# Attention layer of a two-layer decoder trunk: four engines issue in source order instead of the scheduler's order

## Chip, core and metric

The kernel runs on one core of a Trainium2 chip. The metric is the device time of one execution in microseconds (us); smaller is better. Three runs of the kernel before gave 1360.05 to 1361.44 us, median 1360.51 us.

## What is computed

A decoder trunk of two pre-normalised residual layers over one sequence of 512 tokens, D = 1024, each followed by a dense SwiGLU layer. The first layer mixes with a recurrence (a gated linear recurrence beside a state-space mixer), the second with dilated window attention. The change is in the attention layer, which in the reference reads, cut:

```python
def attention_layer(x, norm_g, w_qkv, q_norm, k_norm, w_out):
    h = rmsnorm(x, norm_g)
    qkv = (h @ w_qkv).reshape(b, l, 3, ATT_HEADS, ATT_HEAD_DIM)      # 16 heads of 64
    q = partial_rope(rmsnorm(qkv[:, :, 0], q_norm), pos) * (ATT_HEAD_DIM ** -0.5)
    k = partial_rope(rmsnorm(qkv[:, :, 1], k_norm), pos)
    v = qkv[:, :, 2]
    for window, dilation in DILATED_PATTERNS:                        # (128,1) (512,4) (2048,16)
        o_i, m_i, d_i = dilated_window_attention(q, k, v, window, dilation)
        ...
    o = jnp.sum(wts[..., None] * jnp.stack(outs), axis=0) / jnp.sum(wts, axis=0)[..., None]
    return x + o @ w_out
```

and around it, for layer 0 and 1: `x = mixer(x)`, then `x = x + (silu(g) * u) @ w_down` with `g, u = split(rmsnorm(x) @ w_gate_up)`. Everything is float32. The kernel folds the three windows into one softmax per row over all 512 keys, with a table of logarithmic counts (`lnc`) added to the scores.

## The kernel before, in words

Activations stand transposed, as eight tiles of 128 channels x 512 tokens. Float32 products are made from three matmuls of split operands: every operand is kept as a rounded high part and the rest as a low part (`xh`, `xl`; `wh`, `wl`; `ph`, `pl`; `qk_hi`, `qk_lo`). `split` (L87 to L89) makes such a pair: ACT casts the high part (L88), DVE subtracts it (L89). A weight tile of 128 x 1024 is loaded by SP (L110, three buffers `wr`) and split into `wh` and `wl` (three buffers each), two tiles ahead of its use.

PE does all matmuls, ACT casts, squares and exponentials, DVE most elementwise work, POOL (GpSimd) a few powers and the division of the probabilities. In time the layers are: recurrent layer, its feed-forward layer, attention (about 723 to 1006 us of the profiled execution), second feed-forward layer.

In the attention layer the source is written as a hand-made interleaving. Large projections are cut into *pieces* of about 1.4 us of PE work, kept in the list `pieces`; `fill_in(n)` issues n of them between the small, dependent steps of the heads, and runs what was put off with `later` (so many pieces later) or `after_piece` (after the next fill). Pieces and steps:

- `qk_pieces`: six matmuls `ps_qkv` (L762 to L764) a piece, 16 pieces for four heads' q and k. Their end: ACT `q` and `qsq` (L773, L775); two pieces later DVE `qss` (L784, L785) and POOL `qrs`, a power (L786); six pieces later DVE `q` scaled by `qrs` (L790); seven and eight later the rotary part `rc`, `rs` (L801, L802) and two additions (L806, L807).
- `v_pieces`: twelve matmuls `ps_v` of 256 columns (L827 to L829), 8 pieces; the last four evacuate, ACT `v` (L836) and DVE `v` (L837). `ps_qkv`, `ps_v` and `ps_ao` share four PSUM buffers.
- `pair_T`: PE transposes `ps_qT` (L849), ACT `qk_hi` (L852), DVE `qk_lo` (L853).
- `scores(p, b)`, b = 0, 1, 2: PE `ps_s` (L873), DVE adds `lnc` and takes the row extreme (L884, `s,m`), ACT exponential (L885); then, after the next fill, `quotients`: DVE reciprocal (L890) and POOL's product `s` (L892).
- `turn(h, b)`: PE transposes the probabilities, `ps_pT` (L900), then ACT `ph` and DVE `pl`. `turn(h, 0)` reads all four row blocks of head h and so needs the quotients of all three score groups.
- `values(h, b)`: PE `ps_o` from `pl` (L915) and `ph` (L916); at its end ACT `bot` (L923) and DVE `o` (L926) and the split into `xh`, `xl`.
- `ao_pieces`: output projection, six matmuls `ps_ao` (L117 to L119) a piece, DVE adds to `x` (L950).

The loop runs over eight pairs of heads, p = 0 to 7, twelve steps each: turns and values of the pair (ha, hb), and between them `pair_T` and `scores` of the next pair. Pairs 0 to 4 have twelve pieces, one a step (p = 0, 2, 4: the last four qk pieces of a group and its eight v pieces; p = 1, 3: twelve qk pieces); pairs 5, 6 and 7 have only 4, 5 and 4 `ao` pieces for twelve steps.

Tiles carry the dependences, and semaphores are put in for them. The order in which an engine issues is not that of the source: the scheduler of the tile framework picks, engine by engine, among what is ready by its own estimate. Each engine then issues its own list in that order, and an instruction that waits holds up all that stands behind it on its engine.

Of the kernel before, what the change touches and what calls it, by code (L numbers as in the profile page):

```python
# [25 lines left out]
HID = ((0, 8), (8, 15), (15, 22))  # L26
XBC = 12
NEG = -1e30


_PV = {}
# [27 lines left out]
def trunk(ctx: ExitStack, tc: tile.TileContext, a):  # L59
# [185 lines left out]
    norm = Norm("rec_norm")  # L245
# [11 lines left out]
    with ExitStack() as rctx:  # L257
# [390 lines left out]
        norm = Norm("ffn_norm0", (8, 9, 10, 11, 4, 5, 6, 7))  # L648
# [38 lines left out]
    norm = norm2  # L687
    norm3 = Norm("ffn_norm1", (8, 9, 10, 11, 4, 5, 6, 7))
    with ExitStack() as actx:
# [34 lines left out]
        queue = []  # L724
# [86 lines left out]
        def v_pieces(g):  # L811
            pss = []

            def piece(vp, t):
                i = i_qkv[g, 4 + vp]
                if t == 0:
                    w_cur[i] = weight_get(i)
                if vp == 0:
                    pss.append(pa.tile([P, T], F32, tag="pa", name="ps_v"))
                wh, wl = w_cur[i]  # L820
                ts_ = slice(t * P, (t + 1) * P)
                ps = pss[t][:, :256]
                for k4 in range(4):
                    k = 4 * vp + k4
                    xh, xl = norm.hl[k]
                    cols = slice(k4 * 256, (k4 + 1) * 256)
                    mm(ps, lhsT=xl[:, ts_], rhs=wh[:, cols], start=(k == 0), stop=False)  # L827
                    mm(ps, lhsT=xh[:, ts_], rhs=wl[:, cols], start=False, stop=False)
                    mm(ps, lhsT=xh[:, ts_], rhs=wh[:, cols], start=False, stop=(k == KD - 1))  # L829
                if t == 2:  # L830
                    weight_emit(i + AHEAD)
                if vp == 1:
                    v = ap_.tile([P, 4, 2, 64], F32R, tag=f"v{t}", name="v", bufs=2)
                    r = norm.rt[:, t:t + 1]
                    pv3 = ps.rearrange("p (h e) -> p h e", h=4)
                    S.activation(v[:, :, 0], pv3, AF.Copy, scale=r)  # L836
                    V.scalar_tensor_tensor(out=v[:, :, 1], in0=pv3, scalar=r, in1=v[:, :, 0].bitcast(F32), op0=ALU.mult, op1=ALU.subtract)  # L837
                    vt[g, t] = v

            return [lambda vp=vp, t=t: piece(vp, t) for vp in range(2) for t in range(NT)]  # L840
# [3 lines left out]
        def pair_T(p, w):  # L844
            g, pp = p // 2, p % 2
            o = w * 256 + pp * P
            ps = pm.tile([P, T], F32, tag="pm", name="ps_qT")
            for t in range(NT):
                nc.tensor.transpose(ps[:, t * P:(t + 1) * P], qk[g][:, t].rearrange("p h e -> p (h e)")[:, o:o + P], ident)  # L849
            hi = ap_.tile([P, T], F32R, tag=f"hi{w}", name="qk_hi", bufs=2)  # L850
            lo = ap_.tile([P, T], F32R, tag=f"lo{w}", name="qk_lo", bufs=2)
            S.activation(hi, ps, AF.Copy, scale=gains[w])  # L852
            V.scalar_tensor_tensor(out=lo, in0=ps, scalar=gains[w], in1=hi.bitcast(F32), op0=ALU.mult, op1=ALU.subtract)  # L853
            qkT[p, w] = (hi, lo)
# [9 lines left out]
        def scores(p, b):  # L864
            (qh, ql), (kh, kl) = qkT[p, 0], qkT[p, 1]
            pss = [pm.tile([P, T], F32, tag="pm", name="ps_s") for _ in range(2)]
            for i, c in S_AT[b]:
                n = (i + 1) * P
                qs = slice(i * P, (i + 1) * P)
                for z, (ql_, kr) in enumerate(((qh, kl), (ql, kh), (qh, kh))):  # L870
                    for e in range(2):
                        rows = slice(64 * e, 64 * e + 64)
                        mm(pss[e][:, c:c + n], lhsT=ql_[rows, qs], rhs=kr[rows, :n], start=(z == 0), stop=(z == 2))  # L873
            k = 2 * len(S_AT[b])
            m = am.tile([P, 3, 4], F32, tag="m", name="m", bufs=6)
            done = []
            for i, c in S_AT[b]:
                n = (i + 1) * P
                for e in range(2):
                    if c == 0:  # L880
                        prob[2 * p + e, "s", b] = at.tile([P, WID[b]], F32, tag=f"s{b}", name="s", bufs=4)
                    s, ps = prob[2 * p + e, "s", b][:, c:c + n], pss[e][:, c:c + n]
                    u = len(done)
                    V.tensor_tensor_reduce(out=s, in0=ps, in1=lnc[:, T - n:], scale=-1.0, scalar=-NEG, op0=ALU.add, op1=ALU.min, accum_out=m[:, 0, u:u + 1])  # L884
                    S.activation(s, s, AF.Exp, scale=-1.0, bias=m[:, 0, u:u + 1], accum_out=m[:, 1, u:u + 1])  # L885
                    prob[2 * p + e, i] = s
                    done.append(s)

            def quotients():
                V.reciprocal(m[:, 2, :k], m[:, 1, :k])  # L890
                for u, s in enumerate(done):
                    G.tensor_scalar(out=s, in0=s, scalar1=m[:, 2, u:u + 1], scalar2=1.0, op0=ALU.mult, op1=ALU.mult)  # L892

            after_piece.append(quotients)
# [39 lines left out]
        def ao_pieces(half, after=None):  # L934
            st = {}

            def piece(mp, m2, kk):
                i = i_ao[half, mp]
                if m2 == 0 and kk == 0:
                    w_cur[i] = weight_get(i)  # L940
                if kk == 0:
                    st["ps"] = pa.tile([P, T], F32, tag="pa", name="ps_ao")
                for k in (2 * kk, 2 * kk + 1):
                    c = (m2 * 4 + k) * P
                    mm3(st["ps"], w_cur[i], oT[4 * half + k], (slice(None), slice(c, c + P)), (slice(None), slice(None)), k == 0, k == 3)
                if m2 == 0 and kk == 1:
                    weight_emit(i + AHEAD)
                if kk == 1:
                    m = 2 * mp + m2
                    V.tensor_tensor(out=x[m], in0=st["ps"], in1=x[m], op=ALU.add)  # L950
                    if after is not None:
                        after(m)

            return [lambda mp=mp, m2=m2, kk=kk: piece(mp, m2, kk) for mp in range(4) for m2 in range(2) for kk in range(2)]
# [3 lines left out]
        def fill_in(n=1):  # L958
            for _ in range(min(n, len(pieces))):
                pieces.pop(0)()  # L960
                tick()
            ready = after_piece[:]
            after_piece.clear()
            for f in ready:
                f()


        pieces += qk_pieces(0)
        fill_in(4)
        norm.finish()  # L970
        fill_in(12)
        pieces += v_pieces(0)
        fill_in(8)
        pieces += qk_pieces(1)
        fill_in(2)
        pair_T(0, 0)
        pair_T(0, 1)
        fill_in(3)
        for b in range(3):
            scores(0, b)  # L980
            fill_in(2)
        fill_in(1)
        for p in range(8):
            g = p // 2
            if p % 2 == 0 and g < 3:
                pieces += v_pieces(g + 1)
            elif p % 2 == 1 and g < 2:
                pieces += qk_pieces(g + 2)
            elif p == 5:
                pieces += ao_pieces(0)  # L990
            n = [12, 12, 12, 12, 12, 4, 5, 4][p]
            nxt = p < 7
            ha, hb = 2 * p, 2 * p + 1
            steps = [
                [lambda: turn(ha, 0)],
                [lambda: turn(ha, 1)] + ([lambda: pair_T(p + 1, 0)] if nxt else []),
                [lambda: values(ha, 0), lambda: turn(ha, 2)],
                [lambda: values(ha, 1)] + ([lambda: pair_T(p + 1, 1)] if nxt else []),
                [lambda: values(ha, 2)],
                [lambda: turn(hb, 0)],  # L1000
                [lambda: scores(p + 1, 0)] if nxt else [],
                [lambda: values(hb, 0), lambda: turn(hb, 1)],
                [lambda: scores(p + 1, 1)] if nxt else [],
                [lambda: values(hb, 1), lambda: turn(hb, 2)],
                [lambda: scores(p + 1, 2)] if nxt else [],
                [lambda: values(hb, 2)],
            ]
            for k, fs in enumerate(steps):
                for f in fs:
                    f()  # L1010
                fill_in(n * (k + 1) // 12 - n * k // 12)
        fill_in(len(pieces))
        assert not queue
        pieces += ao_pieces(1, norm3.feed)
        fill_in(len(pieces))

    def store(m):
        nc.sync.dma_start(out=a["out"][m], in_=x[m])
# [98 lines left out]
```

## Time and profile before

| | us |
|---|---|
| median of three runs | 1360.51 |
| the profiled execution | 1360.34 |
| its span, first to last instruction | 1358.5 |
| PE busy | 1323.7 (97%) |
| DVE busy | 779.4 (57%) |
| ACT busy | 553.3 (41%) |
| POOL busy | 74.8 (6%) |
| attention layer, from 723 to 1006 us: PE busy of 283.0 | 266.05 |

PE's share is near the whole span, so time is lost or won where PE stands still or runs at a lower clock. "Idle before <- releaser" in a row is how long the engine had stood, and whose end set it free. The clock column is the granted TensorE clock as a share of 2.4 GHz.

### The profile page before, as it was taken

Reading aid. Unit: us, or ns where it says so; the run is one execution under the profiler, and the core shown is the slowest. Engines: PE = TensorE matmul, PEld = TensorE weight load, DVE = VectorE, ACT = ScalarE, POOL = GpSimd, SP = SyncE. Lnnn points to the kernel's source line nnn. Section 1 sums busy time; section 2 is a strip of 40 time slices with the busy share of each in tenths; the row PEclk is TensorE's granted clock in tenths of the full one; section 3 lists DMA queues with packets and bytes.
Section 4 is the critical chain, followed back from the end, with each engine's and each line's share of the span. In section 5 each row is a group of like instructions: output and inputs, shape, how many; then the busy total and the mean of one; then the engine's idle time right before and its main releaser. Section 6 shows DMA issues by size and latency. Waiting matters only on the chain.

```text
span 1358.5 us, 16006 instructions
## 1 busy us (share of the span) xinstructions
PE 1323.7 (97%) x6314; PEld 1086.0 (80%) x6314; DVE 779.4 (57%) x1264; ACT 553.3 (41%) x818; POOL 74.8 (6%) x94
## 2 busy tenths in 40 slices
PE   7999989999999999999999889989999999999998
PEld 6877767788888888888888778777788888888887
DVE  6887799975544434434465575767754434443442
ACT  6743867433333222222244466556543212222321
POOL 0000000000000000000001232232100000000000
PEclk9999989999999999999999999999999999999999
DMA  6322322532333333332332211211133332233332
GB/s 237 110 89 82 94 78 85 164 95 94 96 94 103 94 93 102 87 107 94 95 97 87 78 48 62 63 47 47 63 93 94 95 106 94 89 97 105 97 90 81
DMA packets 38555, 126.53 MB, mean 93 GB/s; under 512 B 4288, under 2 KB 5056, under 8 KB 38352
## 3 DMA queue, kind: packets, MB, share of 16 engines
q1 hardware_dynamic: 38480, 125.51, 29.9%
q8 instruction: 49, 0.80, 0.2%
q14 instruction: 26, 0.21, 0.0%
HBM read 123.36 MB, written 2.13 MB: 92 GB/s over the span
## 4 chain that ended last, share of the span: by engine, by line
PE 86%; DVE 6%; ACT 4%; POOL 2%; issue 1%; DMA 0%; SPq 0%; POOLq 0%; ACTq 0%; DVEq 0%
PE ps_pr L117 24%; PE ps_pr L118 24%; PE ps_pr L119 24%; PE ps_qkv L762 2%; POOL qrs L786 2%; PE ps_qkv L764 2%; PE ps_qkv L763 2%; PE ps_ao L119 1%; PE ps_ao L117 1%; PE ps_ao L118 1%; DVE wl L89 1%; PE ps_s L873 1%; PE ps_pT L900 1%; ACT s L885 1%; DVE qss L784 1%
## 5 line engine op out<-in xcount | busy, mean ns | idle before, releaser
L88 ACT CAST wh<-wr 128x1024 fp32r<-128x1024 f32 (+2 forms) x223 | 228.3, 1024 | 609.6 <-PE ps_pr L119 389.3
L117 PE MATMUL ps_pr<-xh,wl 128*128 128x512 f32 x1056 | 416.9, 395 | 13.6 <-DVE wl L89 12.1
L118 PE MATMUL ps_pr<-xl,wh 128*128 128x512 f32 x1056 | 414.6, 393 | 0.0
L119 PE MATMUL ps_pr<-xh,wh 128*128 128x512 f32 x1056 | 413.5, 392 | 0.0
L89 DVE TENSOR_TENSOR wl<-wr,wh 128x1024 fp32r<-128x1024 f32 (+2 forms) x223 | 265.3, 1190 | 76.4 <-ACT wh L88 75.6
L117 PEld LDWEIGHTS ps_pr<-xh,wl 128*128 128x128 f32 x1056 | 199.4, 189 | 56.4 <-DVE wl L89 13.0
L119 PEld LDWEIGHTS ps_pr<-xh,wh 128*128 128x128 f32 x1056 | 199.4, 189 | 42.3 <-issue 0.7
L118 PEld LDWEIGHTS ps_pr<-xl,wh 128*128 128x128 f32 x1056 | 199.5, 189 | 42.0 <-issue 1.1
L119 PE MATMUL ps_pr<-ah,wh 128*128 128x512 f32 x352 | 137.1, 389 | 0.0
L117 PE MATMUL ps_pr<-ah,wl 128*128 128x512 f32 x352 | 137.1, 389 | 0.0
L118 PE MATMUL ps_pr<-al,wh 128*128 128x512 f32 x352 | 137.1, 389 | 0.0
L671 DVE TENSOR_TENSOR tu<-ps_pr,nrb 128x512 f32<-128x512 f32 x44 | 30.4, 691 | 130.7 <-PE ps_pr L119 130.7
L679 DVE TENSOR_TENSOR x<-ps_pr,x 128x512 f32<-128x512 f32 x48 | 33.2, 692 | 122.6 <-PE ps_pr L119 122.6
L669 DVE TENSOR_TENSOR tg<-ps_pr,nrb 128x512 f32<-128x512 f32 x44 | 30.4, 691 | 94.0 <-PE ps_pr L119 94.0
L119 PEld LDWEIGHTS ps_pr<-ah,wh 128*128 128x128 f32 x352 | 66.1, 188 | 13.8
L117 PEld LDWEIGHTS ps_pr<-ah,wl 128*128 128x128 f32 x352 | 66.1, 188 | 13.7
L118 PEld LDWEIGHTS ps_pr<-al,wh 128*128 128x128 f32 x352 | 66.1, 188 | 13.6
L762 PE MATMUL ps_qkv<-wh,xl 128*128 128x512 f32 x128 | 54.3, 424 | 3.9 <-DVE v L837 3.9
L885 ACT ACTIVATE s<-s,m 128x512 f32<-128x512 f32 (+3 forms) x64 | 35.4, 554 | 55.3 <-DVE m L884 55.3
L764 PE MATMUL ps_qkv<-wh,xh 128*128 128x512 f32 x128 | 51.0, 398 | 0.0
L763 PE MATMUL ps_qkv<-wl,xh 128*128 128x512 f32 x128 | 50.6, 396 | 0.0
L892 POOL TENSOR_SCALAR s<-s,m 128x512 f32<-128x512 f32 (+3 forms) x64 | 38.4, 616 | 109.9 <-DVE m L890 84.4
(230 smaller groups left out, 1615.7 us busy)
## 6 DMA issues: line engine op xcount, KB each, us to landing
wr<-in_w_gu SPq DMA_DIRECT2D x88, 512.0 KB, 3.5
wr<-in_w_in SPq DMA_DIRECT2D x35, 512.0 KB, 3.6
wr<-in_w_dn SPq DMA_DIRECT2D x32, 448.0 KB, 3.3
wr<-in_w_qkv SPq DMA_DIRECT2D x24, 512.0 KB, 3.5
wr<-in_w_out SPq DMA_DIRECT2D x16, 512.0 KB, 3.5
wr<-in_w_dn SPq DMA_DIRECT2D x16, 512.0 KB, 3.5
x<-in_xT SPq DMA_DIRECT2D x16, 256.0 KB, 3.6
bcs<-csd SPq DMA_DIRECT2D x16, 256.0 KB, 4.6
```

The lines of the kernel that those rows point to most:

```text
L88: S.copy(hi, src)
L89: V.tensor_tensor(out=lo, in0=src, in1=hi.bitcast(F32), op=ALU.subtract)
L117: mm(ps, lhsT=wl[ws], rhs=xh[xs], start=start, stop=False)
L118: mm(ps, lhsT=wh[ws], rhs=xl[xs], start=False, stop=False)
L119: mm(ps, lhsT=wh[ws], rhs=xh[xs], start=False, stop=stop)
L669: V.tensor_tensor(out=tg, in0=pg, in1=rb, op=ALU.mult)
L679: V.tensor_tensor(out=x[m], in0=ps, in1=x[m], op=ALU.add)
L762: mm(pss[t], lhsT=xl[:, ts_], rhs=wh[:, cols], start=(k == 0), stop=False)
L763: mm(pss[t], lhsT=xh[:, ts_], rhs=wl[:, cols], start=False, stop=False)
L764: mm(pss[t], lhsT=xh[:, ts_], rhs=wh[:, cols], start=False, stop=(k == KD - 1))
L885: S.activation(s, s, AF.Exp, scale=-1.0, bias=m[:, 0, u:u + 1], accum_out=m[:, 1, u:u + 1])
L892: G.tensor_scalar(out=s, in0=s, scalar1=m[:, 2, u:u + 1], scalar2=1.0, op0=ALU.mult, op1=ALU.mult)
```

## The change

Inside the attention layer the body that issues all pieces and steps is put into `with tc.manual_schedule(engines=ORDERED)`, where `ORDERED` is PE, ACT, DVE and POOL: these four issue in the order in which the source makes the instructions. SP, which issues the loads, stays with the scheduler. No instruction is added or removed. The lines after it move by one (before the block) or two (inside it).

```diff
+ORDERED = {mybir.EngineType.PE, mybir.EngineType.Activation, mybir.EngineType.DVE, mybir.EngineType.Pool}
...
-        pieces += qk_pieces(0)
-        fill_in(4)
-        norm.finish()
-        fill_in(12)
...
+        with tc.manual_schedule(engines=ORDERED):
+            pieces += qk_pieces(0)
+            fill_in(4)
+            norm.finish()
+            fill_in(12)
...
+            for p in range(8):
...
+            fill_in(len(pieces))
+            assert not queue
+            pieces += ao_pieces(1, norm3.feed)
+            fill_in(len(pieces))
```

The order of POOL and of SP is the same in both kernels. PE's is the same up to pair 5. DVE and ACT move all through the layer.

DVE, pair 0, around the `pl` of `values(1, 0)`, before (`wl_6036` is the low part of the next weight tile, `q` the scaled q of one token block, `s,m` the scores of pair 1):

```order
L926 TENSOR_TENSOR o<-ps_o,bot 64x512
L784 TENSOR_REDUCE qss<-qsq 128x8
L785 TENSOR_SCALAR qss<-qss 128x8
L89 TENSOR_TENSOR wl_6036<-wr_6034,wh_6035 128x1024
L89 TENSOR_TENSOR pl<-ps_pT,ph 128x512
L790 TENSOR_TENSOR q<-q,qrs 128x512
L884 ISA s,m<-ps_s,cst 128x512
```

and after:

```order
L785 TENSOR_REDUCE qss<-qsq 128x8
L786 TENSOR_SCALAR qss<-qss 128x8
L927 TENSOR_TENSOR o<-ps_o,bot 64x512
L90 TENSOR_TENSOR pl<-ps_pT,ph 128x512
L791 TENSOR_TENSOR q<-q,qrs 128x512
L885 ISA s,m<-ps_s,cst 128x512
...
L90 TENSOR_TENSOR wl_6038<-wr_6036,wh_6037 128x1024
L791 TENSOR_TENSOR q<-q,qrs 128x512
```

The weight's low part moved from ahead of `pl` to behind the scores, and each `q` from right behind its own `qss` to behind all four of them.

DVE, end of pair 0, around the last reciprocal of pair 1's scores, before (`128x256` scores are group b = 2):

```order
L837 SCALAR_TENSOR_TENSOR v<-ps_v,nrt,v 128x4x64
L884 ISA s,m<-ps_s,cst 128x256
L884 ISA m 128x1
...
L890 RECIPROCAL m<-m 128x2
L837 SCALAR_TENSOR_TENSOR v<-ps_v,nrt,v 128x4x64
L926 TENSOR_TENSOR o<-ps_o,bot 64x512
```

and after:

```order
L802 TENSOR_TENSOR rc<-q,rope_c 128x512
L803 TENSOR_TENSOR rs_6145<-q,rope_s 128x512
L885 ISA s,m<-ps_s,cst 128x256
L885 ISA m 128x1
...
L90 TENSOR_TENSOR wl_6177<-wr_6175,wh_6176 128x1024
L838 SCALAR_TENSOR_TENSOR v<-ps_v,nrt,v 128x4x64
L807 TENSOR_TENSOR q<-rc,rs_6145 128x32x8
L808 TENSOR_TENSOR q<-rc,rs_6145 128x32x8
L891 RECIPROCAL m<-m 128x2
```

Four instructions now stand between these scores and their reciprocal: a weight's low part, one `v` and the two rotary additions. On ACT the cast of that weight, `wh_6176`, stands behind the two exponentials of the same scores. At the end of the odd pairs 1 and 3 one weight's low part stands there.

PE, pair 5, from the last scores of pair 6 to `values(11, 2)`, before (`ps_ao` are matmuls of the output projection):

```order
L900 MATMUL ps_pT<-cst,s 128x128 x2
L873 MATMUL ps_s<-qk_lo,qk_hi 128x256 x2
L873 MATMUL ps_s<-qk_hi,qk_lo 128x256 x2
L873 MATMUL ps_s<-qk_hi 128x256 x2
L117 MATMUL ps_ao<-xh_6815,wl_7254 128x512
L118 MATMUL ps_ao<-xl_6816,wh_7253 128x512
L915 MATMUL ps_o<-pl,v 128x256
```

and after:

```order
L901 MATMUL ps_pT<-cst,s 128x128 x2
L874 MATMUL ps_s<-qk_lo,qk_hi 128x256 x2
L874 MATMUL ps_s<-qk_hi,qk_lo 128x256 x2
L874 MATMUL ps_s<-qk_hi 128x256 x2
L916 MATMUL ps_o<-pl,v 128x256
L917 MATMUL ps_o<-ph,v 128x256
L118 MATMUL ps_ao<-xh_6817,wl_7256 128x512
```

The two matmuls of the output projection that stood ahead of the values moved behind them.

## Rows read from the trace of the kernel before

**Rows 1.** The page: busy time, share of the span and instructions by engine.

```profile
PE 1323.7 (97%) x6314; PEld 1086.0 (80%) x6314; DVE 779.4 (57%) x1264; ACT 553.3 (41%) x818; POOL 74.8 (6%) x94
```

**Rows 2.** PE's waits from 720 to 1010 us: total, times, longest.

```profile
PE ps_o L915 <- DVE pl L89: 10.9, 6, 3.1
PE ps_qkv L762 <- DVE v L837: 3.9, 1, 3.9
PE ps_s L873 <- DVE qk_lo L853: 1.6, 3, 0.6
```

**Rows 3.** First long stop: DVE, then PE (start, us, operation, idle before).

```profile
752.00 0.69 DVE L790 TENSOR_TENSOR q<-q,qrs 128x512 f32<-128x512 f32 x1 [1.75 <-POOL qrs L786]
...
755.87 1.65 DVE L837 SCALAR_TENSOR_TENSOR v<-ps_v,nrt,v 128x256 fp32r<-128x256 f32 x4
...
756.40 0.51 PE L762 MATMUL ps_qkv<-wh,xl 128*128 128x512 f32 x1 [3.89 <-DVE v L837]
```

**Rows 4.** Stop in pair 0: DVE, then PE; last row: the same in pair 4.

```profile
796.03 0.68 DVE L89 TENSOR_TENSOR pl<-ps_pT,ph 128x512 fp32r<-128x512 f32 x1
...
791.68 0.40 PE L873 MATMUL ps_s<-qk_hi 64*128 64x512 f32 x2
...
796.77 0.50 PE L915 MATMUL ps_o<-pl,v 128*128 128x512 f32 x1 [3.06 <-DVE pl L89]
...
909.86 0.50 PE L915 MATMUL ps_o<-pl,v 128*128 128x512 f32 x1 [2.92 <-DVE pl L89]
```

**Rows 5.** Stretches: length, busy PE, PEld, DVE, ACT, POOL, clock, DMA share, GB/s.

```profile
756.50:760.50 4.00, 4.00 (x11) 3.13 (x12) 2.15 (x4) 0.00 (x0) 0.00 (x0) 0.57 0.63 158
797.50:805.00 7.50, 7.50 (x53) 7.02 (x52) 7.02 (x20) 4.41 (x13) 2.94 (x3) 0.77 0.24 72
...
951.00:955.00 4.00, 3.03 (x22) 2.17 (x18) 2.64 (x12) 3.04 (x12) 1.50 (x3) 1.00 0.00 0
```

**Rows 6.** End of pair 0: DVE, POOL, PE; then DVE busy (x) in a stretch, clock.

```profile
808.71 0.17 DVE L890 RECIPROCAL m<-m 128x2 f32<-128x2 f32 x1 [0.82 <-ACT s L885]
...
808.97 0.93 POOL L892 TENSOR_SCALAR s<-s,m 128x256 f32<-128x256 f32 x2 [1.21 <-DVE m L890]
...
809.45 0.60 PE L900 MATMUL ps_pT<-cst,s 128*128 128x128 f32 x4
...
798.25:809.60 11.35, 9.13 (x30) 0.86 0.23 78
```

**Rows 7.** End of pair 1: the same chain.

```profile
833.68 0.93 POOL L892 TENSOR_SCALAR s<-s,m 128x256 f32<-128x256 f32 x2 [0.39 <-DVE m L890]
...
834.78 0.60 PE L900 MATMUL ps_pT<-cst,s 128*128 128x128 f32 x4
```

**Rows 8.** Groups from 723 to 965 us by shape: busy, mean ns, idle before.

```profile
L88 ACT CAST wh<-wr 128x1024 fp32r<-128x1024 f32 x27 | 28.3, 1046 | 24.0 <-PE ps_qkv L764 18.0 <-PE ps_v L829 3.6 <-issue 1.8
...
L885 ACT ACTIVATE s<-s,m 128x512 f32<-128x512 f32 x16 | 11.4, 716 | 35.2 <-DVE m L884 35.2
...
L885 ACT ACTIVATE s<-s,m 128x256 f32<-128x256 f32 x16 | 8.0, 502 | 7.7 <-DVE m L884 7.7
...
L89 DVE TENSOR_TENSOR wl<-wr,wh 128x1024 fp32r<-128x1024 f32 x27 | 33.2, 1229 | 20.4 <-ACT wh L88 20.1
...
L790 DVE TENSOR_TENSOR q<-q,qrs 128x512 f32<-128x512 f32 x16 | 11.1, 693 | 26.1 <-POOL qrs L786 26.1
L837 DVE SCALAR_TENSOR_TENSOR v<-ps_v,nrt,v 128x256 fp32r<-128x256 f32 x16 | 7.4, 480 | 1.2 <-ACT v L836 1.1
```

**Rows 9.** Pair 5, last scores and values: PE twice, then DVE.

```profile
936.83 0.50 PE L117 MATMUL ps_ao<-xh,wl 128*128 128x512 f32 x1
...
938.28 0.39 PE L915 MATMUL ps_o<-pl,v 128*128 128x256 f32 x1 [0.72 <-DVE pl L89]
...
940.35 0.15 DVE L890 RECIPROCAL m<-m 128x2 f32<-128x2 f32 x1
```

**Rows 10.** DMA issues: weight tiles of the attention layer, KB each, us to landing.

```profile
wr<-in_w_qkv SPq DMA_DIRECT2D x24, 512.0 KB, 3.5
```

More of the change, by code (lines that the diff above doesn't have):

```diff
@@ L965, in fill_in @@
                 f()
-        pieces += qk_pieces(0)
-        fill_in(4)
-        norm.finish()
-        fill_in(12)
[L972 to L980, printed above, removed]
-            fill_in(2)
[L982 to L1015, printed above, removed]
+        with tc.manual_schedule(engines=ORDERED):
[3 more added lines that the diff above has]
+            fill_in(12)
+            pieces += v_pieces(0)
+            fill_in(8)
+            pieces += qk_pieces(1)
+            fill_in(2)
+            pair_T(0, 0)
+            pair_T(0, 1)
+            fill_in(3)
+            for b in range(3):
+                scores(0, b)
+                fill_in(2)
+            fill_in(1)
+            for p in range(8):
+                g = p // 2
+                if p % 2 == 0 and g < 3:
+                    pieces += v_pieces(g + 1)
+                elif p % 2 == 1 and g < 2:
+                    pieces += qk_pieces(g + 2)
+                elif p == 5:
+                    pieces += ao_pieces(0)
+                n = [12, 12, 12, 12, 12, 4, 5, 4][p]
+                nxt = p < 7
+                ha, hb = 2 * p, 2 * p + 1
+                steps = [
+                    [lambda: turn(ha, 0)],
+                    [lambda: turn(ha, 1)] + ([lambda: pair_T(p + 1, 0)] if nxt else []),
+                    [lambda: values(ha, 0), lambda: turn(ha, 2)],
+                    [lambda: values(ha, 1)] + ([lambda: pair_T(p + 1, 1)] if nxt else []),
+                    [lambda: values(ha, 2)],
+                    [lambda: turn(hb, 0)],
+                    [lambda: scores(p + 1, 0)] if nxt else [],
+                    [lambda: values(hb, 0), lambda: turn(hb, 1)],
+                    [lambda: scores(p + 1, 1)] if nxt else [],
+                    [lambda: values(hb, 1), lambda: turn(hb, 2)],
+                    [lambda: scores(p + 1, 2)] if nxt else [],
+                    [lambda: values(hb, 2)],
+                ]
+                for k, fs in enumerate(steps):
+                    for f in fs:
+                        f()
+                    fill_in(n * (k + 1) // 12 - n * k // 12)
+            fill_in(len(pieces))
+            assert not queue
+            pieces += ao_pieces(1, norm3.feed)
+            fill_in(len(pieces))
```

## Prediction
> **What bounds the kernel now.** I read the page first, then PE's waits in the attention layer, then the rows around each long wait, and last the granted clock behind them. PE is busy 97% of the span and no other engine over 80% [rows 1], so the change can win only where PE stands still or runs slowly inside the layer. PE's waits there [rows 2] are few: one of 3.89 us for a DVE `v` [rows 3], six together 10.9 us for a DVE `pl`, three of 0.6 at most for `qk_lo`. Of the six, three are alike, one each in pairs 0, 2 and 4, of 3.06 us at the first and 2.92 at the last [rows 4]; the three others, in pairs 5 to 7, make up the rest, 2.0.
>
> The long ones have one cause. DVE has put each `q` right behind its own `qss`, and must stand 1.75 us for POOL's power in between [rows 3]; `q` waits 26.1 us in its sixteen places [rows 8]. What PE needs, a `v` or a `pl`, stands behind that. DVE itself has time: it is busy 9.13 of 11.35 us even in the dense stretch at the end of pair 0 [rows 6].
>
> They cost more than their idle time. Behind the first stop the granted clock is a mean 0.57 over 4 us, behind the second 0.77 over 7.5 us [rows 5], levels of 0.5 and 1.0 mixed: 4 x 0.43 and 7.5 x 0.23, about 1.7 us of PE work lost each time. Behind the waits below 1 us near 952 us the clock stayed at 1.00 [rows 5].
>
> **What goes.** PE's order is the same up to pair 5, so until there only DVE's and ACT's orders count. With `qss` of all four token blocks ahead and `q` six pieces behind its square, POOL's power is long done when `q` comes: in the first part the `v` stand in their pieces and the 3.89 us stop goes, with its clock: -3.9 - 1.7 = **-5.6 us**. In pairs 0, 2 and 4 `pl` no longer stands behind a waiting `q` and a weight's low part: -3.0 each, with the `qk_lo` wait of about 0.5 just ahead (1.6 in three, rows 2) and the clock 1.7, which is -5.2 each.
>
> **What comes at the end of pairs 0, 2 and 4.** PE's next turn needs the quotients of all three score groups. In the kernel before this chain is met with nothing to spare: reciprocal 808.71, POOL's first product from 808.97 (two in 0.93), PE's transposes at 809.45 with no wait [rows 6]. In the new order DVE does a weight's `wl`, a `v` and two additions ahead of that reciprocal, and the `wh` that `wl` waits for stands on ACT behind the exponentials. That alone adds, by starts of 0.08 less than the means in [rows 8], 0.97 (`wh`) + 1.15 (`wl`) + 0.40 (`v`) + 0.7 (two additions of half a `q`) = 3.2 us, all of it on the path: the low bound, which supposes that DVE comes to the last scores as early as PE does.
>
> It does not. From the first 512-wide score of the next pair PE needs, to its next turn, 809.45 - 791.68 [rows 4, 6] less the stop of 3.06, the 1.7 of clock and about 0.3 for the first head's share: 12.7 us. DVE has from that score to the reciprocal what it had before from 798.25 to 809.60, 9.13 us [rows 6], and besides `wl` 1.15 and three `q` of 0.61 that stood earlier: 12.1 us. In strict order it also waits three times on ACT. The first `wl` waits for a cast behind two exponentials of 512: 0.7 + 2 x 0.72 + 0.97 against 1.2 of its own work, 2 us. The first `v` waits behind four exponentials, about 1.3. The second `wl` waits for two exponentials of 256 (0.50 each, rows 8) and a cast, 1.8. Sum 17.2, POOL's start and first product 0.7 [rows 6]: 17.9 against PE's 12.7. Stop: **about 5 us**, in one piece at the turn, bounds 2.6 (some slack gained ahead) to 6.5. Such a stop is longer than all those behind which the clock halved, so 1.7 goes with it. Net 5.0 + 1.7 - 5.2 = +1.5 each, **+4.5 us** for three; with 2.6 and no clock loss -7.8, with 6.5 and the clock +9.
>
> The Trainium skill ("TensorE: Matmul & The Clock Gate", What's actually happening) says that the gate watches a free-running window, so whether a given idle time costs the clock depends on where it falls. The trace does not show such luck for the long stops of this layer, both stretches of rows 5 lost 1.7; were the three new ones to escape, the sum below would be lower by 5.1.
>
> **The end of pairs 1 and 3.** One `wh` and one `wl` come between the exponentials and the last reciprocal: 0.97 + 1.15 and some 0.07 of handing over, 2.2. Before, POOL starts at 833.68, half of its 0.93 later the first head's product is there, and PE comes at 834.78 [rows 7]: 0.6 to spare. Stop 1.5 each, **+3.0**. Its length lies between waits that did and did not cost the clock [rows 4, 5]; I take none, bounds +2.0 to +6.4 with it.
>
> **Pairs 5 to 7.** With four or five pieces for twelve steps the scheduler had filled PE's gaps with single `ps_ao` matmuls. In source order they are gone. In pair 5 the last values could be reached at 936.83, where the first `ps_ao` of the filling stands, and could start at 938.28 [rows 9]: 1.4 instead of 0.72. Then one piece, 1.4, and the turn at about 939.9, while the reciprocal is at 940.35 [rows 9] and POOL 0.7 behind [rows 6]: 1.2. `values(ha, 0)` comes with only eight transposes of the other turn and `pair_T` between: cast and `pl`, some 0.68 each [rows 4], against two to three groups of four transposes of 0.60 at most [rows 6]: an estimate of 0.5. Pair 6 has a piece ahead of its last values, so 0.5 + 1.2; pair 7 has no `pair_T` and again none, 0.9 + 0.9. Sum 6.6, against 2.0 before: **+4.5**, bounds +2 and +8 (whole pieces may still cover more, or each of these gaps may lengthen the next).
>
> **At nothing.** No instruction is added. The loads stay in SP's order; `wr` is set free up to 3 us later where its cast stands behind exponentials, but a load lands in 3.5 us [rows 10] and is made two tiles, eight pieces or 11 us, ahead. POOL's order is unchanged, and it is 6% busy [rows 1]. If the cover of the loads failed, a weight would be late by about 1 us a tile at the dense ends of pairs.
>
> **Sum.** -5.6 + 4.5 + 3.0 + 4.5 = +6.4 us on the profiled execution's 1360.34, which is 0.17 under the median: 1366.7, and 1366.9 against the median; I say **1367**. The ends of the terms: -5.6 - 7.8 + 2 + 2 = -9.4, 1351; -5.6 + 9 + 6.4 + 8 = +17.8, 1378.
>
> **Rivals.**
> 1. *Faster.* The four long stops go (12.8 us with 6.8 of clock and 1.6 for `qk_lo`, 21 us in all), and the turn at the end of the even pairs waits only for what is put ahead of the reciprocal. For: DVE's busy share is moderate, and its 1.75 us waits for POOL vanish, which may let it reach the last scores early enough. Against: three waits behind ACT in the new order. With stops of 2.6 to 3.2 that keep the clock the three pairs give -7.8 to -6.0, the rest +1.9: 1354 to 1357. It decides below 3.5 us a stop, clock kept. Chance 0.25.
> 2. *No change that can be measured.* What can be told from none is about 0.2%, 2.7 us. The turn's stop with its clock equals the stop that went, 5.2 (three pairs at 0), or the ends of pairs 1 and 3 and pairs 5 to 7 come out at their low bounds, +4: 1358 to 1363. That the change does nothing, since PE's order moves so little, ends here too; but DVE's order moves at just those places where PE waits. Chance 0.17.
> 3. *Much slower.* The shorter new stops cost the clock too, and the stop of the even pairs is 6.5: up to +17.8, 1373 to 1378. It decides if a stop of 1.5 us is enough for the clock to fall. Chance 0.13.
>
> The forecast (1363 to 1373) has 0.45. Faster 0.25, same 0.17, slower 0.58. The range for 8 in 10 takes in most of the faster case and of the slower ones: 1354 to 1375.
>
> **What would show it.** Right: no wait of PE for `v` near 752 us and none of 3 us for `pl`; in their place PE's `ps_pT` waits for POOL's `s` five times, three times about 5 us and twice 1.5, the clock at half behind the three; DVE's reciprocal there right behind two additions; `q` without waits for POOL; PE waits for `pl` four or five times of 0.5 to 1.4 in pairs 5 to 7. Wrong: a wait for `ps_pT` below 3 us in pair 0 (rival 1), PE waits for weights (`wl`), or for `pl` in the middle of an even pair, which would mean that DVE is late already there.

## The result: slower, 1377.5 us, and the profile after

The changed kernel takes 1377.5 us in the median of four runs (1376.36 to 1379.58), against 1360.84 for the kernel before on the same chip: ratio 1.0125, 95% interval 1.0107 to 1.0142. The prediction was 1367 with 1354 to 1375 as its range. The side was right, the size was not: the span grew by 18.3 us (1358.5 to 1376.8), almost three times the +6.4 of the sum, and the time lies outside the range.

The page of the profile after (busy time, share of the span, instructions), to be read beside [rows 1]:

```profile
PE 1331.5 (97%) x6314; PEld 1091.1 (79%) x6314; DVE 781.3 (57%) x1264; ACT 553.9 (40%) x818; POOL 75.9 (6%) x94
```

The instructions are the same. PE's busy time rose by 7.8 us with the same matmuls, which points to a lower clock; the waits and the clock are added up below. PE's waits in the attention layer (total, times, longest), to be read beside [rows 2]:

```profile
PE ps_pT L901 <- POOL s L893: 19.2, 7, 5.2
PE ps_o L916 <- DVE pl L90: 7.6, 7, 2.4
PE ps_s L874 <- DVE m L885: 1.6, 2, 1.4
```

16.7 us of waits before have become 28.5. The long wait for `v` [rows 3] and the three of 3 us for `pl` [rows 4] are gone, and so are those for `qk_lo`. In their place stands the wait of the next pair's turn for POOL's product, just where the prediction put it. The end of pair 0, to be read beside [rows 6] (start, duration, operation, idle before):

```profile
798.79 0.41 DVE L885 CUSTOM_DVE_ANT_0 s<-ps_s,cst 128x256 f32<-128x256 f32 x1
...
801.30 1.23 DVE L90 TENSOR_TENSOR wl<-wr,wh 128x1024 fp32r<-128x1024 f32 x1 [1.75 <-ACT wh L89]
802.44 0.48 DVE L838 SCALAR_TENSOR_TENSOR v<-ps_v,nrt,v 128x256 fp32r<-128x256 f32 x1
802.84 0.42 DVE L807 TENSOR_TENSOR q<-rc,rs 128x256 f32<-128x256 f32 x1
803.17 0.42 DVE L808 TENSOR_TENSOR q<-rc,rs 128x256 f32<-128x256 f32 x1
803.50 0.16 DVE L891 RECIPROCAL m<-m 128x2 f32<-128x2 f32 x1
...
800.24 1.03 ACT L89 CAST wh<-wr 128x1024 fp32r<-128x1024 f32 x1
...
803.83 0.93 POOL L893 TENSOR_SCALAR s<-s,m 128x256 f32<-128x256 f32 x2 [4.03 <-DVE m L891]
...
804.36 0.90 PE L901 MATMUL ps_pT<-cst,s 128*128 128x128 f32 x3 [5.11 <-POOL s L893]
...
833.32 0.55 PE L901 MATMUL ps_pT<-cst,s 128*128 128x128 f32 x3 [1.30 <-POOL s L893]
```

The last row is the end of pair 1. Read the others upwards from 804.36: PE had stood 5.11 us, POOL's product was released by the reciprocal, and the reciprocal stood behind two additions, a `v` and a `wl` that itself waited 1.75 us for its cast on ACT. The ends of pairs 2 and 4 look the same (5.17 and 5.16), those of pairs 1 and 3 have stops of 1.30 each.

Pairs 5 to 7 hold what the prediction missed: PE's longer stops there, then DVE just ahead of one of them:

```profile
936.74 0.32 PE L874 MATMUL ps_s<-qk_lo,qk_hi 64*128 64x128 f32 x1 [1.35 <-DVE m L885]
...
948.72 0.72 PE L916 MATMUL ps_o<-pl,v 128*128 128x512 f32 x1 [1.66 <-DVE pl L90]
...
959.02 0.78 PE L916 MATMUL ps_o<-pl,v 128*128 128x512 f32 x1 [2.44 <-DVE pl L90]
...
972.92 0.80 PE L916 MATMUL ps_o<-pl,v 128*128 128x512 f32 x1 [1.55 <-DVE pl L90]
...
955.95 1.23 DVE L90 TENSOR_TENSOR wl<-wr,wh 128x1024 fp32r<-128x1024 f32 x1 [0.80 <-ACT wh L89]
957.09 0.68 DVE L951 TENSOR_TENSOR x<-ps_ao,x 128x512 f32<-128x512 f32 x1
957.69 0.67 DVE L927 TENSOR_TENSOR o<-ps_o,bot 64x512 f32<-64x512 f32 x1
958.29 0.67 DVE L90 TENSOR_TENSOR pl<-ps_pT,ph 128x512 fp32r<-128x512 f32 x1
```

The `pl` that PE wants at 956.58 (959.02 less 2.44) stands behind a weight's low part, which waits for its cast, and an addition to `x` and an `o` that nobody is waiting for yet. The waits above 0.25 us of pairs 5 to 7 add up to 10.3 us in ten places, against 2.0 before.

The clock, in stretches that begin where a stop ends (the one at 938.40 begins where the clock falls, 1.7 us behind the stop of 1.35): length, busy time by engine, then the granted clock, DMA share, GB/s, to be read beside [rows 5]. The last row is from the kernel before, behind its stop in pair 2:

```profile
804.40:811.40 7.00, 7.00 (x28) 5.90 (x29) 3.08 (x5) 2.41 (x5) 0.36 (x1) 0.68 0.15 60
833.40:836.40 3.00, 3.00 (x19) 2.64 (x20) 1.30 (x2) 2.25 (x4) 0.32 (x1) 1.00 0.63 180
864.60:871.60 7.00, 7.00 (x25) 5.94 (x26) 3.08 (x5) 2.39 (x4) 0.36 (x1) 0.59 0.16 63
...
925.40:932.40 7.00, 7.00 (x38) 6.26 (x39) 3.73 (x7) 3.78 (x7) 0.33 (x1) 0.79 0.14 58
938.40:945.40 7.00, 6.53 (x28) 5.02 (x27) 3.73 (x18) 4.48 (x15) 3.49 (x7) 0.76 0.03 8
948.70:955.70 7.00, 6.98 (x32) 5.68 (x32) 2.40 (x4) 2.70 (x5) 0.00 (x0) 0.76 0.00 0
959.00:966.00 7.00, 6.98 (x35) 5.56 (x36) 3.50 (x14) 3.42 (x11) 1.36 (x2) 0.76 0.16 64
972.90:979.90 7.00, 6.80 (x28) 5.37 (x29) 4.12 (x6) 2.49 (x4) 0.00 (x0) 0.77 0.22 67
...
853.20:860.70 7.50, 7.50 (x52) 6.82 (x53) 6.46 (x19) 3.45 (x9) 3.77 (x3) 0.81 0.24 72
```

Length times what the clock lacks: 2.2, 2.9 and 1.5 us behind the three long stops, nothing behind a stop of 1.30, and 1.6 to 1.7 four times in pairs 5 to 7. That is 13.2 us against 6.6 before (1.7 behind three stops and 1.4 behind the one in pair 2). Idle time 28.5 - 16.7 = 11.8 and clock 6.6 make 18.4, for the 18.3 us measured.

### The profile page after: what moved, and what is told of

It reads as the page before. It is cut to its first block, busy times and chain, and to the rows that moved or that the text cites. A ratio compares the mean times of both kernels' runs of the same rounds, so it can differ in the third digit from the quotient of the medians.

```text
span 1376.8 us, 16001 instructions
## 1 busy us (share of the span) xinstructions
PE 1331.5 (97%) x6314; PEld 1091.1 (79%) x6314; DVE 781.3 (57%) x1264; ACT 553.9 (40%) x818; POOL 75.9 (6%) x94
## 4 chain that ended last, share of the span: by engine, by line
PE 88%; DVE 5%; ACT 5%; issue 1%; POOL 0%; DMA 0%; SPq 0%; ACTq 0%; POOLq 0%; DVEq 0%
PE ps_pr L118 24%; PE ps_pr L119 24%; PE ps_pr L120 23%; PE ps_qkv L763 2%; PE ps_qkv L764 2%; PE ps_qkv L765 2%; ACT s L886 1%; PE ps_pT L901 1%; DVE wl L90 1%; PE ps_ao L118 1%; ACT wh L89 1%; PE ps_ao L119 1%; PE ps_ao L120 1%; PE ps_s L874 1%; PE ps_o L916 1%
## 5 line engine op out<-in xcount | busy, mean ns | idle before, releaser
L901 PE MATMUL ps_pT<-cst,s 128*128 128x128 f32 x160 | 30.1, 303 | 19.3 <-POOL s L893 19.2
```

The lines of the kernel that those rows point to most:

```text
L901: nc.tensor.transpose(ps[:, c + (i - j) * P:c + (i - j + 1) * P], prob[h, i][:, j * P:(j + 1) * P], ident)
```

## Experiments

Theory A: the two halves of the layer are separate, pairs 0 to 4 with the start cost little and pairs 5 to 7 cost 15 us; and each stop has the chain that its rows show. Rivals: B, the lateness of DVE and ACT in pairs 0 to 4 is carried into pair 5; F, in pairs 5 to 7 it is PE's own order alone, not DVE's; C, a repaired chain gives its gain back at the next wait. Differences are given against the changed kernel unless said otherwise, times are medians. The kernel before, run again beside each, gave 1360.2 to 1360.8 us, so a difference below about 1 us tells nothing.

### Source order for one part of the layer

```diff
-        with tc.manual_schedule(engines=ORDERED):
+        with ExitStack() as region:
+            region.enter_context(tc.manual_schedule(engines=ORDERED))
...
                 elif p == 5:
+                    region.close()
                     pieces += ao_pieces(0)
```

> The source order is kept up to the end of pair 4; from pair 5 on the scheduler orders all engines again. Theory A (of the 18.3 us by which the span grew, pairs 5 to 7 hold 14.9: 8.2 of idle time and 6.7 of clock; pairs 0 to 4 and the start hold 3.5): 1362 to 1366 us, or some us less if the scheduler can pull output-projection matmuls into the 5.2 us stop at the end of pair 4; no PE wait for pl above 1 us after 925 us. Theory B (what costs is DVE and ACT running in source order in pairs 0 to 4, so that they are late when pair 5 begins): stays above 1372 us, with waits for pl above 1.5 us in pairs 5 to 7 still there.

Measured: 1358.76 us, ratio to the kernel before 0.9991 (0.9981 to 1.0). PE's waits in the layer:

```profile
PE ps_pT L901 <- POOL s L893: 15.6, 7, 5.2
PE ps_s L874 <- DVE m L885: 0.6, 1, 0.6
PE ps_o L916 <- DVE pl L90: 0.5, 1, 0.5
```

The waits for `pl` above 0.5 us are gone, and the time is far below B's 1372, so B falls. The stop at the end of pair 4, 5.16 in the changed kernel, is 1.52 here, because PE's order is the scheduler's from there on and output-projection matmuls stand in it. That is the "some us less" of the expectation.

The complement, the region entered only at `p == 5`:

> The complement: the scheduler orders pairs 0 to 4, the source order holds from pair 5 on. Theory A: 1360.8 + 14.9 = 1375.7 us (1372 to 1378), the four long stops of the kernel before all there, and in pairs 5 to 7 waits for pl up to 2.4 us with half clock behind several of them. Theory B: 1362 to 1366 us.

Measured: 1374.64 us, ratio 1.0107 (1.009 to 1.0124): +14.4 on the 1360.23 of the kernel before in the same runs. Theory A holds: nearly all of the loss lies in pairs 5 to 7. The two parts, -1.5 and +14.4, do not add up to the whole, +16.7; the stop of 5.16 at the end of pair 4 stands in full in neither run, and is large enough for the difference.

### The chain at the end of a pair

```diff
-            after_piece.append(quotients)
+            quotients()
```

> The changed kernel with the quotients issued right behind the scores in the source, ahead of the next piece and of what it puts off. Theory A (the stops of 5.1 at the ends of pairs 0, 2, 4 and of 1.30 at those of 1 and 3 are the weight's cast and low part, a v and two additions ahead of the last reciprocal): those stops shrink by 3.2 and by 1.30 or more, 1377.5 - 9.6 - 2.6 = 1365 us if the clock still halves behind the rest, 1359 us if not. Rival C (DVE is late anyhow, and now stands idle at each reciprocal until the exponentials end, about 1 us at 24 places): stops of 4 us or more stay, or come back as waits for pl and v, 1373 to 1380 us.

Measured: 1367.5 us, ratio 1.0054 (1.0039 to 1.0069), 10.0 us less. PE's waits:

```profile
PE ps_o L916 <- DVE pl L90: 10.8, 10, 2.4
PE ps_pT L901 <- POOL s L893: 7.3, 5, 2.1
...
PE ps_qT L850 <- DVE q L808: 1.6, 1, 1.6
```

The stops of 5.1 shrank to between 2.02 and 2.06, by 3.1 where the expectation had 3.2 for the four instructions, and those of 1.30 went. The time is 2.5 us above the 1365; new in the rows are a transpose that waits 1.6 for an addition put off, and 3.2 more of waits for `pl`.

```diff
-                if t == 2:
+                if t == 3:
                     weight_emit(i + AHEAD)
```

(in both `qk_pieces` and `v_pieces`)

> The changed kernel with each weight tile of qk and v emitted one piece later (fourth piece of its predecessor instead of the third), so that its cast and low part stand behind the last reciprocal; the v and the two additions stay ahead of it. Theory A: even stops 5.1 - 2.1 = 3.0, odd stops 0: 1377.5 - 6.3 - 2.6 = 1368.6 us, less if the clock is kept. Rival C: no gain, since DVE is bound by its other work, 1374 to 1380 us; or PE waits for a weight (wl), a new wait in the rows.

Measured: 1372.13 us, ratio 1.009 (1.0074 to 1.0105), 5.4 us less. The stops are 3.16, 3.45 and 3.45 where 3.0 was expected, and those of 1.30 went; a wait of 2.72 for `pl` behind the end of pair 4 took part of it back. Both runs agree on what the stop consists of: 2 us of weight, 1 us of `v` and additions, and 2 us by which DVE comes late.

### Pairs 5 to 7

```diff
-                if m2 == 0 and kk == 1:
+                if m2 == 0 and kk == 0:
                     weight_emit(i + AHEAD)
```

> The changed kernel with the weight tiles of the output projection emitted at the first half of a piece pair instead of the second, which takes a cast and a low part from ahead of the scores (pair 5) and of pl (pair 6). Theory A2 (in pairs 5 to 7 what stands ahead of pl and of the scores on DVE in source order, a weight's low part, an x addition, the output's split, makes PE wait, on top of the matmuls that no longer fill): the waits of 1.35 + 0.29 for the scores' buffer in pair 5 fall below 0.5, that of 2.44 in pair 6 falls to 0.5 to 1.3, one or two stretches of half clock go with them: 1371 to 1375 us. Theory F (only the lost filling on PE): no change beyond 1.5 us, 1376 or more.

Measured: 1374.48 us, ratio 1.0104 (1.0089 to 1.0119), 3.0 us less (the two intervals overlap, but all four runs, 1373.56 to 1375.45, lie below those of the changed kernel). Two of PE's stops, in pairs 6 and 7:

```profile
954.43 0.50 PE L916 MATMUL ps_o<-pl,v 128*128 128x512 f32 x1 [0.63 <-DVE pl L90]
...
969.08 0.80 PE L916 MATMUL ps_o<-pl,v 128*128 128x512 f32 x1 [3.88 <-DVE pl L90]
```

The waits of 1.35 and 0.29 have become a single one of 0.25 and the one of 2.44 is 0.63, as expected if the weight's low part made them. But the weight now stands ahead of another `pl`, and the wait of 1.55 has become 3.88. The idle time as a whole hardly moved (27.9 after 28.3, both of stops above 0.25 us); the gain is clock: in pairs 5 to 7 it fell once, around the stop of 3.88, and not four times. So what stood ahead of `pl` decides *where* PE waits.

Which engine's order decides *how much*, the next two runs ask. First `ORDERED = {mybir.EngineType.PE}`:

> Only PE in source order, ACT, DVE and POOL by the scheduler. PE's order differs from that before in pairs 5 to 7 alone. Theory F: the whole loss of pairs 5 to 7 is PE's order, so as e2: 1372 to 1375 us. Theory A2: with pl pulled ahead by the scheduler the loss is about the +4.5 of the prediction with some clock: 1362 to 1369 us. Either way the four long stops of the kernel before are there.

Measured: 1371.52 us, ratio 1.0085 (1.007 to 1.0101), 11.2 above the kernel before. Its waits:

```profile
PE ps_o L916 <- DVE pl L90: 16.5, 11, 3.0
PE ps_pT L901 <- POOL s L893: 4.2, 4, 1.8
```

and the clock, behind the stop of 3.04 in pair 0 and over pairs 5 to 7:

```profile
797.50:805.00 7.50, 7.44 (x59) 6.79 (x60) 6.57 (x20) 3.62 (x9) 3.73 (x3) 1.00 0.23 72
...
926.00:985.00 59.00, 48.47 (x263) 37.50 (x264) 36.81 (x82) 29.66 (x67) 10.30 (x16) 0.97 0.12 36
```

Up to pair 5 PE's long stops are those of the kernel before. In pairs 5 to 7 the stops make 10.9 us, as much as with all four engines in source order (10.3), though DVE's order is the scheduler's. F holds for the idle time; A2, in which the scheduler's order of DVE would cut the loss to that of the prediction with some clock, falls. But F, which gave DVE's order no effect at all, goes too far: with as much idle time the clock of the profiled run lost 1.8 us there (59 x 0.03) and that of the changed kernel 6.6, and the median lies just under F's 1372. That twelve dependent steps with four or five pieces always leave PE something to wait for, as long as its pieces can't be cut up, is the likely reason; no run tests it with more pieces.

Then the opposite, ACT, DVE and POOL in source order and PE by the scheduler:

> ACT, DVE and POOL in source order, PE by the scheduler. Theory F: PE fills its gaps again, no loss in pairs 5 to 7, so like e1 (1358.8) within 3 us. Theory A2: pl comes late all the same and there are too few matmuls to fill with, 1363 to 1370 us. The stops at the ends of pairs 0 and 2 stay above 4 us unless PE finds other matmuls to put there.

Measured: 1348.26 us, ratio 0.9911 (0.9895 to 0.9928): 12.1 us faster than the kernel before and 29.2 faster than the changed kernel, lower than either theory said. The end of pair 0 in this kernel:

```profile
798.77 0.27 PE L901 MATMUL ps_pT<-cst,s 128*128 128x128 f32 x1
798.79 0.48 PE L763 MATMUL ps_qkv<-wh,xl 128*128 128x512 f32 x1
...
802.78 0.50 PE L763 MATMUL ps_qkv<-wh,xl 128*128 128x512 f32 x1 [0.99 <-DVE v L838]
...
803.63 0.93 POOL L893 TENSOR_SCALAR s<-s,m 128x256 f32<-128x256 f32 x2 [4.04 <-DVE m L891]
...
804.17 0.98 PE L901 MATMUL ps_pT<-cst,s 128*128 128x128 f32 x7 [0.19 <-POOL s L893]
```

POOL's product comes as late as in the changed kernel (803.63 against 803.83), and the reason is the same. But PE has matmuls of the next projection in between, and waits 0.99 and 0.19 instead of 5.11. Here the late reciprocal costs PE little, since PE's order is free.

### Repairs, and one engine at a time

The first repair joins three edits: source order up to pair 4, quotients at once, weights of qk and v one piece later.

> Source order up to pair 4, scheduler after it, quotients right behind the scores and weights of qk and v one piece later (e1, e3 and e4 together). Theory A: the ends of pairs 1 and 3 without a stop, those of 0 and 2 with at most 2.0 us, no stop at the start and at pl: from 1358.8 of e1 down by 10 to 18 us, 1341 to 1349 us. Rival C (DVE's waits at the reciprocals come back elsewhere): 1355 us or more.

Measured: 1349.8 us, ratio 0.9923 (0.9908 to 0.9938). Just above the range of theory A; two stops of 2.0 for the turn stay, and a wait of 1.41 for `pl` behind the first is new. C falls in its strong form, here (1355 or more) as in e3 (1373 or more), but each repair gave a part back: the 1.41 here, 1.6 and 3.2 in e3, 2.72 in e4.

Then `ORDERED = {mybir.EngineType.DVE}`:

> Only DVE in source order; PE, ACT and POOL by the scheduler. Theory D (the gain is DVE's: q no longer right behind qss, pl no longer behind it): 1347 to 1352 us, no stop of 3 us or more. If ACT's order is needed too (casts of weights behind the exponentials, ahead of nothing that PE waits for): 1354 us or more.

Measured: **1340.83 us**, ratio 0.9862 (0.9848 to 0.9877): the fastest kernel of this study, 19.5 us below the kernel before in the same runs and below the 1347 to 1352 expected. PE's waits in the layer, then DVE's `wl` and `q` there (busy, mean ns, idle before):

```profile
PE ps_o L916 <- DVE pl L90: 1.3, 2, 0.7
...
PE ps_pT L901 <- POOL s L893: 0.7, 3, 0.2
...
L90 DVE TENSOR_TENSOR wl<-wr,wh 128x1024 fp32r<-128x1024 f32 x30 | 37.3, 1243 | 5.2 <-ACT wh L89 5.2
...
L791 DVE TENSOR_TENSOR q<-q,qrs 128x512 f32<-128x512 f32 x16 | 11.4, 718 | 0.0
```

`q` waits for nothing (26.1 us in [rows 8]) and `wl` 5.2 us in the same stretch (20.4 there), since ACT, by the scheduler, has the casts done before DVE comes to them. No stretch of the layer shows half clock. This is near the sum of what the prediction listed under "what goes". Of what it listed under "what comes" DVE's part is still there: at the end of pair 0 the low part, the `v` and the two additions stand ahead of the reciprocal as in the changed kernel. But the scheduler has moved eight matmuls of the next projection ahead of the turn's last transposes, and PE waits 0.2 us there.

`ORDERED = {mybir.EngineType.Activation}`:

> Only ACT in source order. Theory D: within 3 us of the kernel before (1357 to 1363), its four stops behind v and pl still there. Otherwise, if ACT's order carries part of the gain: below 1356.

Measured: 1347.7 us, ratio 0.9908 (0.9893 to 0.9923), against theory D; it is the other case of the expectation. Pinning ACT changed the order that the scheduler gave DVE. DVE's longest waits in this kernel's attention layer:

```profile
DVE wl L90 <- ACT wh L89: 20.2, 18, 5.2
...
DVE q L791 <- POOL qrs L787: 10.2, 10, 1.8
```

`q` waits 10.2 us for POOL instead of 26.1. That DVE's order is the way by which the gain came is likely, and not shown by a run of its own.

The repairs of e8 on top of e7:

> As e7 (ACT, DVE, POOL in source order, PE by the scheduler), with the quotients right behind the scores and the weights of qk and v one piece later. What is left in e7 are waits of about 1.0 us for v at the ends of pairs 0 and 2 and 1.5 for the turn at that of 4. If they come from the weight's low part and the late reciprocal: 1344 to 1347 us. If PE's scheduler had hidden the reciprocal anyway: within 1.5 us of e7's 1348.3, or above where DVE now idles at the reciprocals.

Measured: 1349.09 us, ratio 0.9917 (0.99 to 0.9933): no gain over the 1348.26 of e7. With PE free, the reciprocal was hidden already.

Last, PE and DVE in source order, ACT and POOL by the scheduler:

> PE and DVE in source order, ACT and POOL by the scheduler. It splits the stop of 5.1 us at the ends of pairs 0, 2 and 4. If ACT's source order holds a large part of it (the weight's cast behind the exponentials, and DVE's earlier waits for such casts): stops of about 2 us there, ends of pairs 1 and 3 without one, pairs 5 to 7 with about 10 us of waits as in e6: 1362 to 1368 us. If DVE's own order makes them: 4.5 us or more at each, 1374 us or more.

Measured: 1364.14 us (1360.24 to 1365.9), ratio 1.0028 (1.0016 to 1.0039), 13.4 less than the changed kernel. The rows are from its fastest run, of 1360.24 us and a mean granted clock of 0.992; the run at the median has 0.988. A stop at the end of pair 0 and one in pair 6, the clock behind each, and DVE ahead of the first:

```profile
800.59 0.55 PE L901 MATMUL ps_pT<-cst,s 128*128 128x128 f32 x3 [2.04 <-POOL s L893]
...
936.07 0.47 PE L916 MATMUL ps_o<-pl,v 128*128 128x512 f32 x1 [2.28 <-DVE pl L90]
...
936.10:943.10 7.00, 6.22 (x36) 4.88 (x36) 4.48 (x7) 2.24 (x4) 0.00 (x0) 1.00 0.03 5
800.60:807.60 7.00, 7.00 (x31) 5.84 (x31) 3.27 (x6) 2.75 (x5) 0.39 (x1) 0.76 0.16 66
...
793.60 0.48 DVE L838 SCALAR_TENSOR_TENSOR v<-ps_v,nrt,v 128x256 fp32r<-128x256 f32 x1 [1.34 <-ACT v L837]
```

The stops at the ends of pairs 0, 2 and 4 are 2.04 to 2.09, those of pairs 1 and 3 are gone. So 3.1 of the 5.1 us went when ACT and POOL were left free: the weight's low part no longer waits for its cast. The other 2.0 stay with DVE in source order; a `v` that waits 1.34 us for ACT and the instructions ahead of the reciprocal are both in them. This split and that of e3 and e4 overlap, since the cast of 1 us counts in both. In pairs 5 to 7 about 11.6 us of waits are left, as F says.

## Why the prediction was right and wrong

- **What goes** (-5.6, and -5.2 in each of pairs 0, 2, 4): right. None of these waits is in the profile after, and e9, where little comes in their place, is 19.5 us faster than the kernel before, near the 21 us that rival 1 counted for them. Only the clock behind the stop in pair 2 was 1.4 and not the 1.7 that the prediction read at two of the four stops and took for all.
- **The ends of pairs 0, 2 and 4**: the stop was right, 5.11 to 5.17 for "about 5", and so was its make-up: 3.1 for the chain ahead of the reciprocal (e3) and 2 by which DVE comes late. The three waits behind ACT that the sum took for this are in the trace of pair 0 at 1.92 for 2 (first `wl`), 1.35 for 1.3 (`v`) and 1.75 for 1.8 (second `wl`). The clock was sized at 1.7 each, and was 2.2, 2.9 and 1.5; the term came out at +6.4 (15.4 idle and 6.6 of clock less 15.6) for +4.5.
- **The ends of pairs 1 and 3**: 1.30 twice for 1.5, clock kept: +2.6 for +3.0.
- **Pairs 5 to 7**: this step failed. It gave +4.5, at most +8; it was 10.3 - 2.0 of idle time and 6.6 of clock, +14.9 (+14.4 in e2). Two things were missing. First, the step followed the filling on PE and counted for each wait only the chain from the transposes to `pl`, not what stands ahead on DVE in the new order: a weight's low part and its cast, an addition to `x`, an `o` and its split. The places that it lists came to 6.2 us in all for its 6.6. The 1.35 and 0.29 for the scores' buffer and the 2.44 for `pl`, 4.1 us together, it does not list, and e5 shows that the weight ahead of them made them, since they fell to 0.25 and 0.63 when it moved. For the even pairs I had walked through DVE's whole order; for these I had not. Yet a better DVE order alone would not have saved the sum: the idle time stayed in e5, and in e6, with DVE's order free, it was 10.9, of which 8.9 in the places listed. So the idle time that PE's fixed order costs there was put too low, and DVE's order says where it falls; why both orders come to 10 or 11 us stays open. Second, the step took no clock loss, from waits below 1 us before; four of the new stops, of 1.35 to 2.44, cost 1.6 to 1.7 each.
- **The claim that only DVE's and ACT's orders count up to pair 5, since PE's is the same**, compared the two orders and was true of them. It hid a large effect: PE's order was the same as before, but no longer fitted to when the others deliver. With the three other engines in source order and PE free (e7), the scheduler put other matmuls into the stops, and the kernel was 29.2 us faster than with PE fixed as well; some 10 of these lie in pairs 0 to 4, by the 1358.76 of e1, where pairs 5 to 7 were the scheduler's already.
- **The rivals**: the median lies in rival 3's window of 1373 to 1378, which had 0.13 and which the range left out above 1375. Its mechanism came half true: shorter stops cost the clock (1.2 GHz, half of full) in pairs 5 to 7, not at the ends of pairs 1 and 3, and the stops of the even pairs stayed at 5.1. Rival 1's saving of 21 us is real, and 19.5 of it came in the one run with DVE alone in source order (e9); its turn without a long stop came by PE's order, not by an earlier reciprocal. The Trainium skill ("TensorE: Matmul & The Clock Gate", What's actually happening) says that the gate watches a free-running window, from which the prediction took it that the cost of an idle time depends on where it falls. The trace agrees that length alone does not set the cost: three stops of 5.11 to 5.17 us cost 1.5 to 2.9 us, and the stop of 3 us in pair 0 cost 1.7 in the kernel before and nothing in e6. That the place in the window is the reason is not shown.

## What to carry to other kernels

When engines are pinned to source order, walk the order of the helping engines for every place where PE will come, also where PE's own order seems to explain the loss: what nobody waits for yet (weights' low parts, output additions) stands in front of what PE needs. Pin an engine alone before pinning several: here DVE alone gained 1.4%, all four lost 1.25%, because PE in the scheduler's hands put other matmuls into the gaps that DVE's fixed order opened. How the 7 us between e9 and e7, where ACT and POOL are pinned as well, divide between these two no run says. And price every new stop, from about 1.3 us on, with and without the clock.

## What the runs showed of the hardware that I had not expected

A stop need not be 3 us long to cost the clock, nor does its length alone decide. In the changed kernel a stop of 1.30 left the granted clock at 1.00, and those of 1.35 to 2.44 in pairs 5 to 7 were followed by 0.76 or 0.77 over 7 us; in e12 a stop of 2.04 was followed by 0.76 and one of 2.28 by 1.00; and in e6 the clock stayed at 1.00 behind a stop of 3.04 that had cost 1.7 us at the same place in the kernel before. After two of the three stops of 5.1 us the clock stayed at its lower level longer than behind the stops of 3 us before: 2.2 and 2.9 us lost instead of 1.4 to 1.7. What tells these cases apart stays open.
